# Convolution and max-pool on one core: whole-bank seeds in step 1, an earlier turn of G1, and step 3's difference ahead of step 2's sum

## The chip, the cores and the metric

The kernel runs on one core of a Trainium2 chip. The metric is the device time of one execution in microseconds (us). The engines are TensorE (PE, with its weight loads as PEld), VectorE (DVE), ScalarE (ACT), GpSimd (POOL) and SyncE (SP), which only issues DMAs here. SBUF is the on-chip working memory and PSUM the memory that TensorE accumulates into, in eight banks.

## The reference, cut to what matters

```python
batch, c_in, h, w, c_out, k = 16, 64, 64, 64, 128, 3      # pool_size 2, float32
x_pad = np.pad(x, ((0, 0), (0, 0), (1, 1), (1, 1)))
conv[b, co] += weight[co, ci, kh, kw] * x_pad[b, ci, kh:kh+h, kw:kw+w]   # over ci, kh, kw
output[b, c, i, j] = max of conv[b, c, 2*i:2*i+2, 2*j:2*j+2]
```

A 3x3 convolution with a border of zeros, 64 channels to 128, and after it the largest value of each 2x2 square.

## The kernel before

**Tiles.** Two images lie in SBUF one above the other: image 0 of a pair in partitions 0 to 63, image 1 in 64 to 127 (`h` is 0 or 1 in the code). The work has 32 steps. A step is 16 rows of such a pair of images, that is 8 pairs of rows, and makes one PSUM bank of 8 x 64 results for each image and each kind of sum. TensorE multiplies 64 rows of weights for the image above and 64 for the image below at the same time, so its matmuls come in pairs.

**Two rows at a time.** The row filter is rewritten so that an even and an odd row of the convolution share a sum. Seven blocks of turned weights are needed for it: the filter's rows G0, G1, G2, their differences D0 and D2, and GM and GP, half of G0 - G1 + G2 and half of G0 + G1 + G2. Each block is made in `wq`, turned by TensorE into a PSUM bank (`T` followed by the block: `turn`, L157, with three or four transposes at L162) and copied to `wt` (`V` followed by the block: `turn_out`, L168, whose lines L173 to L179 say which engine copies).

**Two kinds of steps** (`TYPES`). A K step casts its rows to bf16 (`kx`) and needs their sum by pairs, `ks` (KS, L294, VectorE: both operands in SBUF). A W step takes its float rows (`wx`) and needs three tiles: the difference by pairs, `we` (E, L325: on VectorE for steps 3, 4, 6 and 11, on GpSimd for the others; step 1's in halves Ea and Eb, L346, on VectorE), the differences of neighbours, `wd` (D, L334, GpSimd; step 1's in halves Da and Db, L361), and the sum by pairs, `ws` (WS, L308 as a reduction or L316 as an addition, VectorE). Each step has for each image an accumulator `ta` and an accumulator `tb`:

- K: PA1 and PA2 go to `ta`, PB1 and PB2 to `tb`. EV copies `ta` to SBUF (`ev`, L392, ScalarE). MX takes the maximum of `tb` and `ev` into `tb` (L420, VectorE). Then PR adds the product of `ks` to `tb`.
- W: P2 (with `we`) goes to `ta`. SE, the seed, copies `ta` to `tb` (L404, ScalarE). P0 goes on to `ta` and P3 to `tb` (both with `wd`). EV copies `ta`, negated (L394). MX takes the maximum, and P1 adds the product of `ws`.
- Both: OD copies the odd columns to SBUF (L424, ScalarE), CM takes the maximum of the even and the odd columns (L430, VectorE), and the store of a step is issued on SP.

The first two steps are cut in halves of four rows. F stands for step 0's products, and G for step 1's: G.0.0 and G.0.1 are the two halves of its P2, G.1 its P0 and G.2 its P3. Step 1's seeds are made in halves as well (SEa and SEb: `seed_half`, L406, with the copy at L416).

**Order.** Nothing is scheduled by a program: the string `ORDER` (L487) lists the steps one after the other, and each engine executes its own in that order. An entry is a name, a step and an image (KS.2, MX.1.0). A product waits in a queue until the other image has one too, and then the two are issued in turns. Banks come from a list, `free`; a bank is freed when its tile has been copied out. GpSimd's sums and differences are held by an added dependency (`on_gpsimd`, L78) until the last VectorE instruction that was noted ahead of them in `ORDER` (`on_vector`, L74: KS, E on VectorE, additions of WS and the like) has ended:

```python
def on_gpsimd(inst):
    behind(inst, sbuf_op[0])
    return inst
```

The first loads are issued at the start, the others by L, LB (SP) and LK (GpSimd) in `ORDER`.

Of the kernel before, what the change touches and what calls it, by code (L numbers as in the profile page):

```python
# [11 lines left out]
def kernel(  # L12
# [9 lines left out]
    nc = tc.nc  # L22
# [11 lines left out]
    R = HO // NQ  # L34
# [9 lines left out]
    WSTEPS = [s for s in range(N) if TYPES[s] == "W"]  # L44
# [17 lines left out]
    acc = [psum.tile([128, R, W], FP32, name=f"acc_{i}") for i in range(8)]  # L62
    free = deque(range(8))
    unset = set(range(8))
# [60 lines left out]
    zeros = const.tile([128, 512], BF16)  # L125
# [10 lines left out]
    D0, G2, D2, G0, G1, GM, GP = BLOCKS.values()  # L136
# [14 lines left out]
    def turned_cols(m):  # L151
        lo = BLOCKS[m] - (m in LEADING)
        hi = BLOCKS[m] + 3
        tp = acc[turned[m]].rearrange("p a b -> p (a b)").bitcast(BF16)
        return lo, hi, tp[:, 0 : (hi - lo) * CO]
# [12 lines left out]
    def turn_out(m):  # L168
        free.append(turned[m])
        lo, hi, src = turned_cols(m)  # L170
        dst = wt[:, lo:hi, :].rearrange("p a b -> p (a b)")
        if m == "GM":
            nc.scalar.mul(dst, src, 0.5)  # L173
        elif m == "GP":
            nc.vector.tensor_scalar_mul(out=dst, in0=src, scalar1=0.5)
        elif m in ("G0", "G1", "G2"):
            nc.scalar.copy(out=dst, in_=src)
        else:
            nc.vector.tensor_copy(out=dst, in_=src)  # L179
# [32 lines left out]
    ta, tb = {}, {}  # L212


    def take(where, s, h, fresh=True):
        t = next((t for t in free if fresh or t not in unset), free[0])
        free.remove(t)
        where[s, h] = t
        return t
# [134 lines left out]
    def wd_half(part):  # L354
        s = WSTEPS[0]
        if part == 0:
            row["wd", s] = d_pool.tile([128, 2 * R, W], BF16, name="wd")
        t, f = wx_rows(s)
        lo, hi = f + R * part, f + R * (part + 1)
        on_gpsimd(  # L360
            nc.gpsimd.tensor_tensor(  # L361
                out=row["wd", s][:, R * part : R * (part + 1), :],
                in0=t[:, lo + 1 : hi + 1, :],
                in1=t[:, lo - 1 : hi - 1, :],
                op=SUB,
            )
        )
# [35 lines left out]
            )  # L403
        nc.scalar.copy(out=acc[t], in_=acc[ta[s, h]])  # L404

    def seed_half(part, h):  # L406
        s = WSTEPS[0]
        span = slice(R // 2 * part, R // 2 * (part + 1))
        if part == 0:
            t = take(tb, s, h, fresh=False)  # L410
            if t in unset:
                unset.discard(t)
                nc.tensor.matmul(
                    acc[t], zeros[:, 0:128], zeros, start=True, stop=True, skip_group_check=True
                )
        nc.scalar.copy(out=acc[tb[s, h]][:, span, :], in_=acc[ta[s, h]][:, span, :])  # L416

    def rowmax(s, h):
        t = acc[tb[s, h]]
        nc.vector.tensor_tensor(out=t, in0=t, in1=ev[s, h], op=MAX)  # L420
# [27 lines left out]
    def cast_more(first):  # L448
# [24 lines left out]
        "Eb": lambda: we_half(1),  # L473
        "Da": lambda: wd_half(0),
        "Db": lambda: wd_half(1),
        "SEa": lambda h: seed_half(0, h),
        "SEb": lambda h: seed_half(1, h),
        "KS": ks, "WS": ws, "E": we, "D": wd, "L": wload, "LB": late_load, "LK": lk,
        "SE": seed, "EV": evac, "MX": rowmax, "OD": odd, "CM": colmax,
    }  # L480
    for m in BLOCKS:
        steps["T" + m] = lambda m=m: turn(m)
        steps["V" + m] = lambda m=m: turn_out(m)
    for m in PRODUCTS:
# [1 line left out]

    ORDER = """  # L487
        D0 g2 TD0 g0 D2 GS TG2 g1 VD0 PR.0.1 XEa TD2 VG2 PA1.2.1 TG0 F.2.0 VD2 XOa LB.3 LB.4 LB.6 LB.8 LB.9
        GM VG0 F.3.0 XOb F.0.0 F.1.0 TGM F.0.1 PA2.2.1 XEb LK.0.0 F.1.1 F.2.1 F.3.1 VGM GP
        Ea KS.0 Eb EV.0.1 G.0.0 EV.0.0 TG1 VG1 G.0.1 P2.3.1 SEa.0 SEa.1 SEb.1 MX.0.1 Da Db TGP SEb.0 MX.0.0 VGP  # L490
        LK.0.1 X2 PR.0.0 G.1.0 X1 G.2.0 PB1.2.1 PB2.2.1 WS.1 G.2.1 G.1.1 L.11 P0.3.1 PA1.2.0 PA2.2.0 P3.3.1
        OD.0.0 OD.0.1 EV.1.0 KS.2 E.3 CM.0.1 EV.1.1 P1.1.1 D.3 CM.0.0 PR.2.1 PB1.2.0 P2.3.0 MX.1.0 PB2.2.0
        EV.2.1 P1.3.1 SE.3.1 EV.2.0 WS.3 MX.1.1 P1.1.0 SE.3.0 P0.3.0 MX.2.0 MX.2.1 EV.3.1 PR.2.0 EV.3.0 D.4
        MX.3.1 OD.2.0 PA1.5.1 OD.1.0 E.4 PA1.5.0 PA2.5.0 P3.3.0 OD.1.1 OD.2.1 L.12 L.14 PA2.5.1 OD.3.1
        P2.4.1 CM.1.1 CM.2.0 P2.4.0 CM.1.0 PA1.7.1 D.6 EV.5.0 CM.3.1 CM.2.1 MX.3.0 PA2.7.1 PB1.5.1 SE.4.0
# [92 lines left out]
```

## Time and profile before

| | |
|---|---|
| median of 3 runs | 104.4 us (104.28 to 104.41) |
| the profiled execution | 104.27 us |
| its span, first to last instruction | 102.5 us |
| mean granted TensorE clock | 0.989 |
| busy: PE, DVE, ACT, POOL | 94%, 90%, 80%, 73% of the span |

A line of the profile's timeline has the start in us from the beginning of the span, the length in us, the engine, the line of the kernel, the operation, the tile written and the tiles read, their shapes, and the number of instructions that are merged in it. In brackets stands the idle time of the engine ahead of it and what ended that. "x2" lines reach from the start of the first to the end of the last. TensorE's ends are modelled, so its starts are the better measure. Consecutive instructions of an engine overlap a little: the next one starts up to 0.1 us before the end of the last.

### The profile page before, as it was taken

Reading aid. Unit: us, or ns where it says so; the run is one execution under the profiler, and the core shown is the slowest. Engines: PE = TensorE matmul, PEld = TensorE weight load, DVE = VectorE, ACT = ScalarE, POOL = GpSimd, SP = SyncE. Lnnn points to the kernel's source line nnn. Section 1 sums busy time; section 2 is a strip of 40 time slices with the busy share of each in tenths; the row PEclk is TensorE's granted clock in tenths of the full one; section 3 lists DMA queues with packets and bytes.
Section 4 is the critical chain, followed back from the end, with each engine's and each line's share of the span. In section 5 each row is a group of like instructions: output and inputs, shape, how many; then the busy total and the mean of one; then the engine's idle time right before and its main releaser. Section 6 shows DMA issues by size and latency. Waiting matters only on the chain.

```text
span 102.5 us, 2545 instructions
## 1 busy us (share of the span) xinstructions
PE 96.8 (94%) x908; PEld 62.7 (61%) x908; DVE 92.5 (90%) x178; ACT 82.3 (80%) x182; POOL 74.8 (73%) x61
## 2 busy tenths in 40 slices
PE   6989999999999999999999999999999999999930
PEld 2476544555865465587777885556745888865500
DVE  1498799999999999999999999999989999987970
ACT  5638988896689997993887898987899899598740
POOL 6227579764995899998999997969997928990000
PEclk9999999999999999999999999999999999999995
DMA  2999999999999999998878995097899451116044
GB/s 67 300 353 266 367 318 289 396 406 343 195 211 310 294 329 308 319 345 210 173 188 252 255 363 187 20 205 265 191 164 225 138 184 51 51 51 203 8 156 151
DMA packets 13421, 23.34 MB, mean 228 GB/s; under 512 B 1120, under 2 KB 9568, under 8 KB 13408
## 3 DMA queue, kind: packets, MB, share of 16 engines
q1 hardware_dynamic: 12400, 20.68, 62.0%
q0 software_dynamic: 864, 2.36, 14.0%
q8 instruction: 7, 0.11, 0.5%
q10 hardware_dynamic: 144, 0.13, 0.4%
q14 instruction: 6, 0.05, 0.1%
HBM read 17.14 MB, written 8.39 MB: 249 GB/s over the span
## 4 chain that ended last, share of the span: by engine, by line
PE 91%; DVE 2%; ACT 2%; issue 1%; DVEq 0%
PE acc L193 86%; PE acc L545 3%; PE acc L162 1%; DVE acc L420 1%; ACT acc L416 1%; ACT od L424 1%; ACT ev L394 0%; DVE wt L179 0%; DVE o L430 0%; DVE kx L446 0%; DVEq L583 0%
## 5 line engine op out<-in xcount | busy, mean ns | idle before, releaser
L193 PEld LDWEIGHTS <-wt 64*128 64x128 bf16 x876 | 60.1, 94 | 31.5 <-issue 1.9
L334 POOL TENSOR_TENSOR wd<-wx 128x1024 bf16<-128x1024 f32 x20 | 47.0, 2356 | 8.3 <-PE acc L193 3.4
L193 PE MATMUL acc<-kx,wt 64*128 64x504 bf16 (+6 forms) x288 | 50.2, 356 | 0.4 <-DVE kx L446 0.4
L193 PE MATMUL acc<-wd,wt 64*128 64x504 bf16 (+3 forms) x264 | 50.0, 367 | 0.2 <-ACT acc L416 0.2
L420 DVE TENSOR_TENSOR acc<-acc,ev 128x512 f32<-128x512 f32 x64 | 41.9, 691 | 1.5 <-PE acc L193 0.8
L193 PE MATMUL acc<-we,wt 64*128 64x512 bf16 (+2 forms) x132 | 31.9, 367 | 0.0
L193 PE MATMUL acc<-ws,wt 64*128 64x504 bf16 (+1 forms) x126 | 28.7, 377 | 0.2 <-DVE acc L420 0.2
L424 ACT COPY od<-acc 128x256 f32<-128x256 f32 x64 | 22.7, 379 | 6.3 <-PE acc L193 5.8
L394 ACT ACTIVATE ev<-acc 128x512 f32<-128x512 f32 x42 | 25.0, 609 | 2.4 <-PE acc L193 2.1
L430 DVE TENSOR_TENSOR o<-acc,od 128x256 f32<-128x256 f32 x64 | 24.7, 416 | 1.1 <-ACT od L424 0.9
L404 ACT COPY acc<-acc 128x512 f32<-128x512 f32 x40 | 23.0, 581 | 3.0 <-PE acc L193 1.7
L325 POOL TENSOR_TENSOR we<-wx 128x512 bf16<-128x512 f32 x16 | 20.2, 1269 | 3.3 <-DVE ws L316 2.4
L193 PE MATMUL acc<-ks,wt 64*128 64x504 bf16 (+1 forms) x66 | 16.5, 377 | 0.1
L308 DVE TENSOR_REDUCE ws<-wx 128x512 bf16<-128x1024 f32 x12 | 14.8, 1231 | 0.0
L392 ACT COPY ev<-acc 128x512 f32<-128x512 f32 x22 | 12.9, 595 | 0.7 <-PE acc L193 0.7
L316 DVE TENSOR_TENSOR ws<-wx 128x512 bf16<-128x512 f32 x9 | 6.7, 763 | 0.0
L294 DVE TENSOR_TENSOR ks<-kx 128x512 bf16<-128x512 bf16 x11 | 4.6, 426 | 0.5 <-ACT kx L453 0.5
L96 POOL DMA_DIRECT2D kx<-in_x_dram x6 | 3.5, 588 | 1.8 <-DVE kx L446 1.8
L545 PE MATMUL acc<-const-bfloat16-1.0 128*128 128x512 bf16 x8 | 3.6, 628 | 0.8 <-PEq L569 0.8
L361 POOL TENSOR_TENSOR wd<-wx 128x512 bf16<-128x512 f32 x2 | 2.5, 1264 | 0.8 <-DVE we L346 0.8
L325 DVE TENSOR_TENSOR we<-wx 128x512 bf16<-128x512 f32 x4 | 2.7, 683 | 0.0
L460 DVE TENSOR_TENSOR wq<-wraw 128x192 bf16<-128x192 f32 x1 | 0.5, 500 | 2.4 <-DMA wraw<-in_weight_dram 2.4
(29 smaller groups left out, 20.1 us busy)
## 6 DMA issues: line engine op xcount, KB each, us to landing
out_dram<-o SPq DMA_DIRECT2D x26, 256.0 KB, 5.0
wx<-in_x_dram SPq DMA_DIRECT2D x10, 512.0 KB, 7.1
wx<-in_x_dram SPq DMA_DIRECT2D x5, 544.0 KB, 7.5
wx<-in_x_dram SPq DMA_DIRECT2D x5, 480.0 KB, 7.5
out_dram<-o SPq DMA_DIRECT2D x11, 128.0 KB, 2.0
kx<-in_x_dram POOLq DMA_DIRECT2D x2, 528.0 KB, 7.8
ksecond<-in_x_dram SPq DMA_DIRECT2D x1, 512.0 KB, 6.2
kx<-in_x_dram POOLq DMA_DIRECT2D x2, 256.0 KB, 7.0
```

Source lines behind the costliest of these rows:

```text
L193: nc.tensor.matmul(acc[t][:, i0:i1, o0:o1], wt[lo : lo + CI, m0 + kw - h, :], rows(lo, i0, i1, c0, c1), start=start and kw == 1, stop=True ...
L308: nc.vector.tensor_reduce(out=row["ws", s], in_=t[:, f : f + 2 * R, :].rearrange("p (r two) w -> p r w two", two=2), axis=mybir.AxisListTy ...
L316: nc.vector.tensor_tensor(out=row["ws", s], in0=t[:, f : f + 2 * R : 2, :], in1=t[:, f + 1 : f + 2 * R : 2, :], op=ADD)
L325: inst = (nc.vector if vector else nc.gpsimd).tensor_tensor(out=row["we", s], in0=t[:, f : f + 2 * R : 2, :], in1=t[:, f + 1 : f + 2 * R : ...
L334: nc.gpsimd.tensor_tensor(out=row["wd", s], in0=t[:, f + 1 : f + 1 + 2 * R, :], in1=t[:, f - 1 : f - 1 + 2 * R, :], op=SUB)
L392: nc.scalar.copy(out=ev[s, h], in_=acc[t])
L394: nc.scalar.mul(ev[s, h], acc[t], -1.0)
L404: nc.scalar.copy(out=acc[t], in_=acc[ta[s, h]])
L420: nc.vector.tensor_tensor(out=t, in0=t, in1=ev[s, h], op=MAX)
L424: nc.scalar.copy(out=od[s, h], in_=acc[tb[s, h]][:, :, 1::2])
L430: nc.vector.tensor_tensor(out=ot[s][:, h], in0=acc[t][:, :, 0::2], in1=od[s, h], op=MAX)
L545: nc.tensor.matmul(acc[n].rearrange("p a b -> p (a b)"), ones[:, 0:128], ones, start=True, stop=True, skip_group_check=True)
```

## The change

Three things change.

1. Step 1's seeds copy a whole bank (SE.1.0, SE.1.1 with `seed`) where they copied two halves each; `seed_half` and its two entries go.
2. TG1, the turn of G1, stands next to TGM, ahead of most of step 0's F products, and not between the two halves of step 1's P2. Its copy to `wt`, VG1, is VectorE's and no longer ScalarE's, and stands behind Eb.
3. E.3 stands directly behind EV.1.0, and KS.2 behind CM.0.0. So the order on VectorE is E.3, CM.0.1, CM.0.0, KS.2, where it was KS.2, E.3, CM.0.1, CM.0.0. D.3 on GpSimd keeps its place between the two CM, and is still held until E.3's end.

TensorE has the same instructions as before, VectorE one more, ScalarE three fewer, and GpSimd and SP keep theirs in the same order. D.4, which was held behind E.3, is now held behind KS.2. Three banks (88, 89 and 90) change places with each other from step 1's P2 on.

```diff
@@ turn_out
-        elif m in ("G0", "G1", "G2"):
+        elif m in ("G0", "G2"):
             nc.scalar.copy(out=dst, in_=src)
         else:
             nc.vector.tensor_copy(out=dst, in_=src)
@@
-    def seed_half(part, h):
-        s = WSTEPS[0]
-        span = slice(R // 2 * part, R // 2 * (part + 1))
-        if part == 0:
-            t = take(tb, s, h, fresh=False)
...
-        nc.scalar.copy(out=acc[tb[s, h]][:, span, :], in_=acc[ta[s, h]][:, span, :])
@@ steps
-        "SEa": lambda h: seed_half(0, h),
-        "SEb": lambda h: seed_half(1, h),
@@ ORDER
-        GM VG0 F.3.0 XOb F.0.0 F.1.0 TGM F.0.1 PA2.2.1 XEb LK.0.0 F.1.1 F.2.1 F.3.1 VGM GP
-        Ea KS.0 Eb EV.0.1 G.0.0 EV.0.0 TG1 VG1 G.0.1 P2.3.1 SEa.0 SEa.1 SEb.1 MX.0.1 Da Db TGP SEb.0 MX.0.0 VGP
+        GM VG0 F.3.0 XOb F.0.0 F.1.0 TGM TG1 F.0.1 PA2.2.1 XEb LK.0.0 F.1.1 F.2.1 F.3.1 VGM GP
+        Ea KS.0 Eb VG1 EV.0.1 G.0.0 EV.0.0 G.0.1 P2.3.1 SE.1.0 SE.1.1 MX.0.1 Da Db TGP MX.0.0 VGP
         LK.0.1 X2 PR.0.0 G.1.0 X1 G.2.0 PB1.2.1 PB2.2.1 WS.1 G.2.1 G.1.1 L.11 P0.3.1 PA1.2.0 PA2.2.0 P3.3.1
-        OD.0.0 OD.0.1 EV.1.0 KS.2 E.3 CM.0.1 EV.1.1 P1.1.1 D.3 CM.0.0 PR.2.1 PB1.2.0 P2.3.0 MX.1.0 PB2.2.0
+        OD.0.0 OD.0.1 EV.1.0 E.3 CM.0.1 EV.1.1 P1.1.1 D.3 CM.0.0 KS.2 PR.2.1 PB1.2.0 P2.3.0 MX.1.0 PB2.2.0
```

More of the change, by code (lines that the diff above doesn't have):

```diff
@@ L404, in seed @@
         nc.scalar.copy(out=acc[t], in_=acc[ta[s, h]])
-    def seed_half(part, h):
-        s = WSTEPS[0]
-        span = slice(R // 2 * part, R // 2 * (part + 1))
-        if part == 0:
-            t = take(tb, s, h, fresh=False)
[L411 to L416, printed above, removed]
     def rowmax(s, h):
```

## The prediction

> **What bounds the kernel now.** I read the page's busy shares and chain first, then the chain in order of time, then the timelines of TensorE, VectorE, ScalarE and GpSimd from 7 to 18 us, where every edit lies.
>
> From the page, the busy shares and the chain; then a piece of the chain in order of time (start, length, what):
>
> ```profile
> PE 96.8 (94%) x908; PEld 62.7 (61%) x908; DVE 92.5 (90%) x178; ACT 82.3 (80%) x182; POOL 74.8 (73%) x61
> PE 91%; DVE 2%; ACT 2%; issue 1%; DVEq 0%
> ...
> 11.31 64.26 PE acc L193 x604
> ```
>
> From 11.31 us on, TensorE is the chain for 64 us without a break, and for another 20 us after a gap of 0.02. So a wait of TensorE gained or lost before about 20 us reaches the end one for one, as long as nothing later waits on something that doesn't shift with it. Two such waits stand in the opening: for VectorE's maxima at 10.30 and for ScalarE's seeds at 11.31. TensorE's timeline (start, length, engine, line):
>
> ```profile
> 8.66 0.49 PE L193 MATMUL acc<-we,wt 64*128 64x256 bf16 x6
> 9.09 0.34 PE L162 MATMUL acc<-ident,wq 128*128 128x128 bf16 x3
> 9.36 0.50 PE L193 MATMUL acc<-we,wt 64*128 64x256 bf16 x6
> 9.80 0.40 PE L162 MATMUL acc<-ident,wq 128*128 128x128 bf16 x4
> 10.30 0.82 PE L193 MATMUL acc<-ks,wt 64*128 64x512 bf16 x6
> 11.31 1.49 PE L193 MATMUL acc<-wd,wt 64*128 64x256 bf16 x24 [0.18 <-ACT acc L416]
> ```
>
> The same stretch of VectorE, and under it GpSimd:
>
> ```profile
> 8.95 1.30 DVE L420 TENSOR_TENSOR acc<-acc,ev 128x512 f32<-128x512 f32 x2 [0.39 <-PE acc L193]
> 10.23 0.42 DVE L175 TENSOR_SCALAR wt<-acc 128x512 bf16<-128x512 bf16 x1
> 10.57 1.24 DVE L308 TENSOR_REDUCE ws<-wx 128x512 bf16<-128x1024 f32 x1
> 12.33 0.42 DVE L294 TENSOR_TENSOR ks<-kx 128x512 bf16<-128x512 bf16 x1 [0.52 <-ACT kx L453]
> 12.67 0.68 DVE L325 TENSOR_TENSOR we<-wx 128x512 bf16<-128x512 f32 x1
> 13.28 0.75 DVE L430 TENSOR_TENSOR o<-acc,od 128x256 f32<-128x256 f32 x2
> 13.94 0.69 DVE L420 TENSOR_TENSOR acc<-acc,ev 128x512 f32<-128x512 f32 x1
> 14.54 1.23 DVE L308 TENSOR_REDUCE ws<-wx 128x512 bf16<-128x1024 f32 x1
> 15.69 2.51 DVE L420 TENSOR_TENSOR acc<-acc,ev 128x512 f32<-128x512 f32 x4
> ```
>
> ```profile
> 13.45 4.67 POOL L334 TENSOR_TENSOR wd<-wx 128x1024 bf16<-128x1024 f32 x2 [1.78 <-DVE we L325]
> ```
>
> The order matters here: KS.2 (12.33) runs while GpSimd computes nothing, E.3 follows, and only E.3's end lets D.3 start at 13.45.
>
> **The opening: the turn of G1 and the seeds.** Pairs of 256 columns start 0.11 us apart (twelve from 7.34 to 8.66). TG1 between G.0.0 and G.0.1 makes the way from one to the other 0.70 us (8.66 to 9.36) where three pairs take 0.33, so taking it out saves 0.37. Next to TGM it adds three transposes at 0.06 (four take 0.40, three 0.34), 0.17. The F products thus end 0.17 later, G.0.1 starts at 8.66 + 0.17 + 0.33 = 9.16, not 9.36, and TGP 0.20 earlier.
>
> The first maximum waits for the last F product: 8.95 becomes 9.12, the two end at 10.25 + 0.17 = 10.42, and PR.0 starts 0.05 later as now, at 10.47. VG1 on VectorE costs nothing there: after Eb (8.14 + 0.42 = 8.56) the engine idles until 8.95, later 9.12, and a copy of this shape from PSUM takes 0.33 (at 5.54). The bound from the other side: GpSimd's Da starts at 8.65, beside it. But VD0's copy ran under GpSimd's GS (4.82, 0.42 us) and VGP under Db (10.23, 0.42), both of the same length, so I take 0.33. Without that cover VG1 would push PR.0 by up to 0.33.
>
> On ScalarE VG1's 0.48 goes, and four half copies (1.30) become two whole ones: 1.06, as two evacuations of the same shape take 1.07. The seeds start 0.59 after G.0.1 starts (9.36 to 9.95), so at 9.75, and end at 10.81. G.1.0 no longer waits for them but for PR.0's three pairs, 0.65 us (17.20 to 17.85): 10.47 + 0.65 = 11.12 instead of 11.31. Gain of the opening: 0.19 us.
>
> **E.3 ahead of KS.2.** VectorE now runs VGP at 10.40, WS.1 at 10.74, and the next starts 1.15 after it (14.54 to 15.69): E.3 at 11.89, not 12.67, ending 12.57. Its rows are issued at 6.10 and take 5.5 us to land, 11.6: in time by 0.3. D.3 waits for E.3 alone and starts 0.09 after it, as now: 12.66, ending 15.01 (2.35). CM.0.1 and CM.0.0 follow E.3 at 12.49 (0.61 after its start, as now). Their odd columns are there: ScalarE's casts follow the seeds at 10.71 (0.10 before their end, as at 11.15 now), the copies of the odd columns start 1.04 after that (11.15 to 12.19) and take 0.66, until 12.41. KS.2's turn comes at 12.49 + 0.66 = 13.15, and then GpSimd is in the middle of D.3.
>
> KS.2 reads two operands in SBUF. What the trace shows of such an instruction when it comes to its turn under a GpSimd TENSOR_TENSOR (VectorE rows, then the GpSimd rows they fell under):
>
> ```profile
> 66.69 0.49 DVE L294 TENSOR_TENSOR ks<-kx 128x512 bf16<-128x512 bf16 x1
> 77.78 1.05 DVE L316 TENSOR_TENSOR ws<-wx 128x512 bf16<-128x512 f32 x1
> ```
>
> ```profile
> 65.62 1.28 POOL L325 TENSOR_TENSOR we<-wx 128x512 bf16<-128x512 f32 x1
> 75.93 2.35 POOL L334 TENSOR_TENSOR wd<-wx 128x1024 bf16<-128x1024 f32 x1
> ```
>
> Alone, L294 takes 0.42 and L316 0.68. Here they take 0.07 and 0.37 more, with 0.21 and 0.50 us of GpSimd's instruction still to run. A third (L316 at 73.69, 0.85 us) takes 0.17 more with 0.30 to run. In each case the excess is that remainder less about 0.13: they end 0.28 (L294) and 0.55 (L316) after GpSimd's end, as if they had stood still until 0.13 before it. At half speed the one at 77.78 would have lost at most 0.25. Maxima (one operand in PSUM) and TENSOR_REDUCE (one operand) under the same GpSimd instructions keep their lengths, 0.69 and 1.23. So KS.2's excess lies between 0.37, the longest that a row shows, and the whole rest of D.3 less 0.13, 1.72. I take the second, because the three rows follow the remainder and not a fixed price: KS.2 ends at 15.01 + 0.28 = 15.29.
>
> The Trainium skill, "SBUF — State Buffer", section "Who interferes with whom", says that a VectorE instruction with two SBUF inputs contends with a GpSimd one that reads SBUF, and that the one that comes second is blocked fully, not throttled. By it the sum is the same, 105.5; by the longest wait shown alone it would be 104.2. The trace agrees as far as its rows go; none holds for longer than 0.37.
>
> Behind KS.2 on VectorE stand the maxima. MX.1.0 starts 0.08 before KS.2's end, at 15.21 (now 13.94); then by the present spacings (0.60, 1.15, 0.60) WS.3 15.81, MX.1.1 16.96, MX.2.0 17.56, ending 18.25. TensorE: P1.1.1 needs MX.1.0's bank. Its turn is 15.87 - 0.19 = 15.68, and it gets it at 15.90 + 0.05 = 15.95: a wait of 0.27. PR.2.0, now at 17.20, comes up 1.33 later, at 17.28, and needs MX.2.0: 18.25 + 0.05 = 18.30, a wait of 1.02. After it the other two maxima end at 18.85 and 19.47, ahead of their readers (18.95, 19.60), so no third wait.
>
> **What else moves.** D.3's reader, P0.3.1, has its rows at 15.01 instead of 15.80, worth nothing, as it stands in the same pair as P1.1.1. D.4 is now held until KS.2's end and starts at 15.38 (now 15.77): no loss. E.4, two SBUF operands too, comes at 19.4, clear of D.4's end at 17.7. D.6 follows E.4 and runs until 22.5, and KS.7, at 21.26 + 1.10, meets its last 0.1: nothing. The store of step 0 and L.12 and L.14 behind it on SP go 0.8 earlier; GpSimd's own DMA issues keep their place up to LK.0.1 and shift with VectorE afterwards. Loads in flight get readers that come 1.1 later. Banks 88 to 90 swap names only.
>
> **Sum:** -0.19 + 0.27 + 1.02 = +1.10 us. The profiled execution took 104.27 with a span of 102.5, so 105.37 with 103.6; it lay 0.13 under the median of 104.40, so the forecast is 105.5.
>
> **Rivals.** (A) KS.2 is held little: not slower. If it ends by 14.00, held under 0.43 us, MX.2.0 is ready when TensorE's turn comes at 17.01, and only the opening's gain is left: 104.40 - 0.19 = 104.2. For it: no row shows a longer hold than 0.37. Against it: all three follow the remainder. 0.06.
>
> (B) Part is given back later. VectorE is busy 90% and TensorE 94%, and TensorE has small waits near the end. Against it: these follow VectorE and ScalarE instructions that follow TensorE itself, and none is for a landing. Half given back: 104.95. 0.09.
>
> (C) E.3's rows land later than 11.89, and VectorE stands there with the whole chain behind it, one for one. For it: the margin is 0.3 us, where it was 1.1, and the next load took 6.4 us, which here would be 12.5, +0.6, 106.1. Against it: nothing ahead of that issue changes. 0.07.
>
> (D) The forecast, 105.5, 0.78. Its own spread is the maxima's start (0.1) and what 80 us of shifted overlaps between VectorE's sums and GpSimd add or spare (0.2): 105.2 to 105.8.
>
> **The numbers.** The range 104.9 to 105.9 takes D, B and the smaller half of C, and leaves out A and the rest. 0.2% is 0.21 us, about what a measurement of this kernel can tell from no change. A lies on that border and is split, 0.03 and 0.03, and 0.01 each is added for what I have not seen: faster 0.04, same 0.04, slower 0.92.
>
> **What would show it.** In the profile after: KS.2 as an L294 row of about 2.1 us from 13.15 that ends 0.28 after D.3; D.3 starting near 12.7; PR.0 at 10.47 and the first wd products at 11.12; TensorE idle shortly before 18.3, released by VectorE's maximum, and the chain passing there through VectorE and GpSimd. A KS.2 of 0.4 to 0.8 us makes A right and the forecast wrong; E.3 starting after 12 with a landing as its releaser is C.

## The result, and the profile after

The changed kernel is slower. Its median is 105.33 us (105.19 to 105.83, 6 runs) against 104.39 (104.25 to 104.42, 6 runs); the ratio is 1.0103, with a 95% interval of 1.0082 to 1.0124. The profiled execution took 105.33 us with a span of 103.6, 1.06 more than that of before.

The page's busy shares and chain, and a piece of the chain in order of time (start, length, what), all of after:

```profile
PE 96.8 (93%) x908; PEld 63.7 (62%) x908; DVE 94.2 (91%) x179; ACT 81.5 (79%) x179; POOL 74.8 (72%) x61
PE 79%; DVE 10%; DMA 4%; issue 2%; ACT 1%; SPq 0%; DVEq 0%
...
11.92 0.60 DVE we L325
12.51 0.70 DVE o L418 x2
13.22 2.02 DVE ks L294
...
18.25 58.39 PE acc L193 x537
```

TensorE is busy as long as before (96.8 us), so nothing was added to its work. The chain now passes through VectorE, from 9.15 to 18.21 us, where before it was TensorE's from 11.31 on. Its longest piece there is KS.2. The same stretch in VectorE's timeline, then GpSimd's (the line numbers behind `seed_half` are 12 lower):

```profile
11.84 0.68 DVE L325 TENSOR_TENSOR we<-wx 128x512 bf16<-128x512 f32 x1
12.46 0.76 DVE L418 TENSOR_TENSOR o<-acc,od 128x256 f32<-128x256 f32 x2
13.13 2.10 DVE L294 TENSOR_TENSOR ks<-kx 128x512 bf16<-128x512 bf16 x1
15.16 0.69 DVE L408 TENSOR_TENSOR acc<-acc,ev 128x512 f32<-128x512 f32 x1
15.76 1.23 DVE L308 TENSOR_REDUCE ws<-wx 128x512 bf16<-128x1024 f32 x1
16.91 2.48 DVE L408 TENSOR_TENSOR acc<-acc,ev 128x512 f32<-128x512 f32 x4
```

```profile
12.61 2.35 POOL L334 TENSOR_TENSOR wd<-wx 128x1024 bf16<-128x1024 f32 x1 [1.14 <-DVE we L325]
15.32 2.37 POOL L334 TENSOR_TENSOR wd<-wx 128x1024 bf16<-128x1024 f32 x1 [0.37 <-DVE ks L294]
```

KS.2, 0.42 us long before, is a row of 2.10 us. It comes to its turn half a microsecond after D.3's start (12.61) and ends 0.29 after D.3 does, by the trace; its operation and its shapes are the same. D.4 (15.32) now waits for it. TensorE's timeline, with the wait that follows:

```profile
10.51 0.82 PE L193 MATMUL acc<-ks,wt 64*128 64x512 bf16 x6 [0.48 <-DVE acc L408]
11.15 1.49 PE L193 MATMUL acc<-wd,wt 64*128 64x256 bf16 x24
...
15.90 0.37 PE L193 MATMUL acc<-ws,wt 64*128 64x512 bf16 x1
...
18.25 0.37 PE L193 MATMUL acc<-ks,wt 64*128 64x512 bf16 x1 [0.88 <-DVE acc L408]
```

The first wd products start at 11.15 and not at 11.31, so the opening did gain. PR.2.0 starts at 18.25 and not at 17.20, behind the maximum of its bank.

### The profile page after: what moved, and what is told of

Its sections match the earlier page's. It is cut to its first block, busy times and chain, and to the rows that moved or that the text cites. A ratio compares the mean times of both kernels' runs of the same rounds, so it can differ in the third digit from the quotient of the medians.

```text
span 103.6 us, 2545 instructions
## 1 busy us (share of the span) xinstructions
PE 96.8 (93%) x908; PEld 63.7 (62%) x908; DVE 94.2 (91%) x179; ACT 81.5 (79%) x179; POOL 74.8 (72%) x61
## 4 chain that ended last, share of the span: by engine, by line
PE 79%; DVE 10%; DMA 4%; issue 2%; ACT 1%; SPq 0%; DVEq 0%
PE acc L193 79%; DVE acc L408 4%; DMA kfirst<-in_x_dram 4%; DVE ks L294 2%; DVE ws L308 1%; DVE o L418 1%; ACT od L412 1%; DVE we L325 1%; ACT ev L394 0%; PE acc L162 0%; DVE kx L434 0%; SPq L110 0%; DVEq L569 0%; DVE wt L175 0%; DVEq L408 0%
## 5 line engine op out<-in xcount | busy, mean ns | idle before, releaser
L193 PEld LDWEIGHTS <-wt 64*128 64x128 bf16 x876 | 61.1, 94 | 31.7 <-issue 3.4
L404 ACT COPY acc<-acc 128x512 f32<-128x512 f32 x42 | 24.1, 582 | 3.4 <-PE acc L193 1.7
L294 DVE TENSOR_TENSOR ks<-kx 128x512 bf16<-128x512 bf16 x11 | 6.3, 576 | 0.0
```

The costliest lines, as they stand in the source:

```text
L193: nc.tensor.matmul(acc[t][:, i0:i1, o0:o1], wt[lo : lo + CI, m0 + kw - h, :], rows(lo, i0, i1, c0, c1), start=start and kw == 1, stop=True ...
L294: nc.vector.tensor_tensor(out=row["ks", s], in0=t[:, f : f + 2 * R : 2, :], in1=t[:, f + 1 : f + 2 * R : 2, :], op=ADD)
```

## The experiments

The theory: KS.2 reads two operands in SBUF and stands still as long as GpSimd's D.3 runs. The rivals: the loss comes with the turn of G1 and the seeds, which put VectorE's maxima later; or with E.3's place; or any VectorE instruction at that place would be held.

TGM starts at 7.01 to 7.14 us in six of the ten profiles and at 7.39 to 7.53 in the other four (KS.2 back ahead, KS.2 with one operand, D.3 behind KS.2, D.3 in halves). The difference arises ahead of everything that was changed: in those four TensorE works at about half its later pace until 6.4 to 6.6 us, with the pairs of F 0.18 to 0.22 us apart, and 0.11 from then on; in the others the pairs are 0.11 apart from the first or the second on. In three of the four the profiled execution is also 0.28 to 0.32 us above the median of its kernel. So the table counts from the start of TGM. "First wd" is G.1.0's first matmul, and "last product" is TensorE's last matmul. KS.2's end is given against D.3's, negative where KS.2 ends first. The ratios are of execution times, with all that varies in them.

| kernel | first wd | KS.2, length | KS.2's end minus D.3's | PR.2.0 | last product | ratio to before (95%) |
|---|---|---|---|---|---|---|
| before | 4.30 | 0.42 | -3.04 | 10.19 | 91.05 | 1 |
| after | 4.09 | 2.10 | +0.29 | 11.19 | 92.09 | 1.0103 (1.0082 to 1.0124) |
| KS.2 back ahead | 4.09 | 0.42 | -3.04 | 9.98 | 90.87 | 0.9983 (0.9971 to 0.9995) |
| the order alone | 4.30 | 1.57 | +0.29 | 11.14 | 92.00 | 1.0084 (1.0065 to 1.0102) |
| KS.2 with one operand | 4.09 | 1.21 | -0.62 | 10.29 | 91.23 | 1.0023 (1.0010 to 1.0035) |
| D.3 behind KS.2 | 4.09 | 0.42 | -2.44 | 9.98 | 90.91 | 0.9985 (0.9968 to 1.0002) |
| D.3 in halves | 4.09 | 1.02 | +0.28 (its first half) | 10.10 | 91.04 | 1.0023 (1.0000 to 1.0046) |
| whole seeds alone | 3.93 | 0.42 | -3.05 | 9.92 | 90.80 | 0.9975 (0.9959 to 0.9991) |
| the turn alone | 4.09 | 0.42 | -3.18 | 9.98 | 90.88 | 0.9997 (0.9985 to 1.0009) |
| the turn in the gap | 3.93 | 0.42 | -3.04 | 9.82 | 90.68 | 0.9980 (0.9963 to 0.9997) |

### KS.2 back ahead of E.3

```diff
-        OD.0.0 OD.0.1 EV.1.0 E.3 CM.0.1 EV.1.1 P1.1.1 D.3 CM.0.0 KS.2 PR.2.1 ...
+        OD.0.0 OD.0.1 EV.1.0 KS.2 E.3 CM.0.1 EV.1.1 P1.1.1 D.3 CM.0.0 PR.2.1 ...
```

> The changed kernel with KS.2 back ahead of E.3; the turn of G1 and the whole-bank seeds stay. Hold theory (KS.2 stood still under D.3 until 0.13 us before its end): KS.2 is a row of 0.42 us near 11.93, E.3 starts at 12.27 and D.3 at 13.04, TensorE waits nowhere between 11.15 and 20 us, and only the opening's gain is left, 0.16 us by the trace of after (11.31 to 11.15): 104.2 us. Rival (the loss came with the turn of G1 or the seeds, which put VectorE's maxima 0.2 later): it stays, 105.3 us.

Measured: 104.27 us, ratio 0.9983 (0.9971 to 0.9995). VectorE's row of KS.2:

```profile
12.36 0.42 DVE L294 TENSOR_TENSOR ks<-kx 128x512 bf16<-128x512 bf16 x1
```

The whole loss is gone with this one move, and the opening's gain appears in the time. That rules out the turn and the seeds as its cause.

### The order alone, in the kernel before

```diff
-        OD.0.0 OD.0.1 EV.1.0 KS.2 E.3 CM.0.1 EV.1.1 P1.1.1 D.3 CM.0.0 PR.2.1 ...
+        OD.0.0 OD.0.1 EV.1.0 E.3 CM.0.1 EV.1.1 P1.1.1 D.3 CM.0.0 KS.2 PR.2.1 ...
```

> The kernel before with E.3 ahead of KS.2 and nothing else changed. Hold theory: E.3 at 11.72, D.3 at 12.49 to 14.84, KS.2 comes up near 13.6, under D.3, and ends at 15.12, the first of step 1's maxima starts at 15.04, that of step 2 ends at 18.08, and PR.2.0 starts at 18.13 and not at 17.20: +0.93, 105.3 us, the same as the whole change, so that the opening's gain is hidden behind the hold. Rival (parts add up: -0.16 from the opening and the rest from the order): 105.5 us. Rival (no hold): 104.4 us.

Measured: 105.29 us, ratio 1.0084. VectorE's row of KS.2 and GpSimd's row of D.3:

```profile
13.66 1.57 DVE L294 TENSOR_TENSOR ks<-kx 128x512 bf16<-128x512 bf16 x1
```

```profile
12.60 2.35 POOL L334 TENSOR_TENSOR wd<-wx 128x1024 bf16<-128x1024 f32 x1 [1.12 <-DVE we L325]
```

Here KS.2 comes up half a microsecond later than in after, and its row is half a microsecond shorter; both end 0.29 after D.3 by the trace. So it is the end of D.3 that counts and not a fixed price. PR.2.0 is as late as in after, within 0.05, although the opening gained nothing: the hold hides what the opening gives.

### KS.2 with one operand

Step 2's K sum as a reduction over pairs of rows, as the float rows of some W steps are summed; the same sums, at the same place. As it is not noted by `on_vector`, D.4 is held until E.3's end and no longer until KS.2's.

```diff
+        if s == 2:
+            with nc.allow_low_precision("bf16 operand of TensorE, as the other row sums"):
+                nc.vector.tensor_reduce(
+                    out=row["ks", s],
+                    in_=t[:, f : f + 2 * R, :].rearrange("p (r two) w -> p r w two", two=2),
+                    axis=mybir.AxisListType.X,
+                    op=ADD,
+                )
+            return
```

> The changed kernel with KS.2 as a reduction over pairs (one operand in SBUF, the same sums), at the same place under D.3. Hold theory (only two operands in SBUF are held): a row near 1.23 us from 13.13, as the reductions of the float rows, not held; step 1's first maximum at 14.28, step 2's ends at 17.32, PR.2.0 at 17.37 where 17.04 would be its turn: -0.16 + 0.33 = +0.17, 104.6 us, though the instruction itself is 0.8 us longer. Rival (whatever VectorE runs with two reads of bf16 rows under D.3 is held): a row of about 2.9 us that ends 1.1 after D.3, and 106.2 us.

Measured: 104.65 us, ratio 1.0023 (1.0010 to 1.0035). VectorE's row, and GpSimd's D.3 and D.4 as one row; KS.2 lies under the first:

```profile
13.61 1.21 DVE L295 TENSOR_REDUCE ks<-kx 128x512 bf16<-128x1024 bf16 x1
```

```profile
13.08 4.68 POOL L343 TENSOR_TENSOR wd<-wx 128x1024 bf16<-128x1024 f32 x2 [1.49 <-DVE we L334]
```

An instruction three times as long, with one operand, ends 0.62 before D.3, and the kernel is faster with it than with the short one with two (104.65 and 105.33 us). This is the run that tells the hold from the rival that anything at that place is held. The reduction is also another operation; that this isn't what counts is shown by the rows of after, where CM.0.0 has the operation of KS.2 (TENSOR_TENSOR) but one of its operands in PSUM: it starts at 12.80, under D.3, and takes 0.41 us. So of what VectorE runs there, only the instruction with two operands in SBUF is held.

### D.3 behind KS.2

```diff
-        OD.0.0 OD.0.1 EV.1.0 E.3 CM.0.1 EV.1.1 P1.1.1 D.3 CM.0.0 KS.2 PR.2.1 ...
+        OD.0.0 OD.0.1 EV.1.0 E.3 KS.2 CM.0.1 EV.1.1 P1.1.1 D.3 CM.0.0 PR.2.1 ...
```

> The changed kernel with KS.2 directly behind E.3, so that D.3 is held until KS.2 has ended; E.3 is still first. Hold theory: KS.2 0.42 us at 12.43, D.3 from 12.94 to 15.29, ahead of its reader's turn at 15.71, no wait of TensorE: 104.2 us, as with KS.2 back ahead. Rival (E.3 ahead is the trouble, since it stands for its rows or delays the odd columns' maxima): 104.5 us or more.

Measured: 104.22 us, ratio 0.9985 (0.9968 to 1.0002). GpSimd's row of D.3 and D.4, the first now released by KS.2:

```profile
13.32 4.67 POOL L334 TENSOR_TENSOR wd<-wx 128x1024 bf16<-128x1024 f32 x2 [1.78 <-DVE ks L294]
```

E.3 stays ahead of KS.2, and the hold is gone; PR.2.0 stands where it stands with KS.2 back ahead. So E.3's place is not the trouble: what costs is that D.3 was let go while VectorE still had an instruction with two operands to come.

### D.3 in halves

```diff
+        if s == 3:
+            for lo in (f, f + R):
+                on_gpsimd(
+                    nc.gpsimd.tensor_tensor(
+                        out=row["wd", s][:, lo - f : lo - f + R, :],
+                        in0=t[:, lo + 1 : lo + 1 + R, :],
+                        in1=t[:, lo - 1 : lo - 1 + R, :],
+                        op=SUB,
+                    )
+                )
+            return
```

> The changed kernel with D.3 as two instructions of half the rows (1.26 us each, as step 1's), the rest as it is. Hold theory (a hold lasts until 0.13 before the end of the GpSimd instruction that is running, and then VectorE's has its turn): first half 12.61 to 13.87, KS.2 comes up at 13.13 and ends at 14.15, a row of 1.0 us; the second half runs after it, to about 15.4, ahead of its reader's turn at 15.71; step 1's first maximum at 14.07, step 2's ends at 17.11 and PR.2.0 starts at 17.16 where 17.04 would be its turn: -0.16 + 0.12, 104.4 us, no change. Rival (the second half, already queued, goes ahead of KS.2): KS.2 still ends after 15.2, and 105.4 us.

VectorE's KS.2, then GpSimd's two halves as one row, from the timeline; the last line is from the view of GpSimd's line L336 (shortest, median and longest, in ns):

```profile
13.47 1.02 DVE L294 TENSOR_TENSOR ks<-kx 128x512 bf16<-128x512 bf16 x1
```

```profile
12.94 2.67 POOL L336 TENSOR_TENSOR wd<-wx 128x512 bf16<-128x512 f32 x2 [1.44 <-DVE we L325]
```

```profile
L336 POOL TENSOR_TENSOR wd<-wx x2: 1266/1352/1437, 12.9 to 14.2; 128x512 bf16<-128x512 f32 x2
```

The row is 1.02 us, as expected: KS.2 waited for the first half only, and went ahead of the second, which was queued. Counted from TGM, PR.2.0 lies 0.09 earlier than in before, and the last product 0.02 earlier: no change, as expected. The time agrees less well: 104.66 us where 104.4 was expected, ratio 1.0023 (1.0000 to 1.0046), with executions from 104.10 to 105.33. In the profiled one (104.61) the excess over before's (104.27) comes from TensorE's slower start: its TGM comes 0.38 later, ahead of all that was changed here. What made the executions above 105 us so long is not settled.

### The parts of the opening

Whole-bank seeds alone, in the kernel before:

```diff
-        ... TG1 VG1 G.0.1 P2.3.1 SEa.0 SEa.1 SEb.1 MX.0.1 Da Db TGP SEb.0 MX.0.0 VGP
+        ... TG1 VG1 G.0.1 P2.3.1 SE.1.0 SE.1.1 MX.0.1 Da Db TGP MX.0.0 VGP
```

> The kernel before with the whole-bank seeds alone; the turn of G1, its copy on ScalarE, and KS.2 ahead of E.3 as before. If the opening's limit is ScalarE's chain: VG1 ends at 9.95, the two seeds at 11.01 (1.06 in place of 1.30), and the first wd products start at 11.07 in place of 11.31, as PR.0 still starts at 10.30: -0.24, 104.2 us. Rival (seeds are off the path, the gain was the turn's): 104.4 us.

Measured: 104.12 us, ratio 0.9975 (0.9959 to 0.9991). TensorE's two rows, and ScalarE's seeds:

```profile
10.38 0.83 PE L193 MATMUL acc<-ks,wt 64*128 64x512 bf16 x6
11.03 1.59 PE L193 MATMUL acc<-wd,wt 64*128 64x256 bf16 x24
```

```profile
10.04 1.06 ACT L404 COPY acc<-acc 128x512 f32<-128x512 f32 x2
```

The first wd product gains more than I expected, 0.37 and not 0.24 counted from TGM: it starts right behind PR.0, at 11.03, while the second seed ends only at 11.10. Of this, 0.26 to 0.27 are left at PR.2.0 and at the last product. A whole-bank seed lets image 0's products start when its own bank is copied; with halves in the order a.0, a.1, b.1, b.0, image 0 was released last. Whether halves with image 0's first would do the same was not run.

The turn of G1 and VG1 on VectorE alone, in the kernel before:

```diff
-        elif m in ("G0", "G1", "G2"):
+        elif m in ("G0", "G2"):
@@
-        ... F.1.0 TGM F.0.1 ... Ea KS.0 Eb EV.0.1 G.0.0 EV.0.0 TG1 VG1 G.0.1 ...
+        ... F.1.0 TGM TG1 F.0.1 ... Ea KS.0 Eb VG1 EV.0.1 G.0.0 EV.0.0 G.0.1 ...
```

> The kernel before with the turn of G1 next to that of GM and VectorE's copy alone; half-bank seeds, and KS.2 ahead of E.3 as before. PR.0 starts at 10.50 as in after (the F products and the maxima are 0.2 later), the four half copies end near 11.08, and the first wd products start at 11.15 in place of 11.31, by PR.0 and no longer by the seeds: -0.16, 104.25 us. With the whole-bank seeds (KS.2 back ahead) it was 104.27, so the whole seeds would add nothing to the turn. Rival (the parts add up: whole seeds 0.24 of which the turn gives none): 104.4 us.

Measured: 104.36 us, ratio 0.9997 (0.9985 to 1.0009). In the trace the first wd products are 0.21 earlier, counted from TGM, just as with both parts (4.09 in both), so the whole seeds add nothing once the turn has moved. Nor does the earlier turn add anything to the whole seeds: the first wd products are at 3.93 with the seeds alone and at 4.09 with both, as PR.0 then waits for the later F products and maxima. The last product is 0.18 earlier than in before, but the time can't tell this gain from none.

### The turn in TensorE's gap

```diff
-        D0 g2 TD0 g0 D2 GS TG2 g1 VD0 PR.0.1 XEa TD2 VG2 PA1.2.1 TG0 F.2.0 VD2 ...
-        GM VG0 F.3.0 ...
+        D0 g2 TD0 g0 D2 GS TG2 g1 VD0 PR.0.1 XEa TD2 VG2 PA1.2.1 TG0 TG1 F.2.0 VD2 ...
+        GM VG0 VG1 F.3.0 ...
-        ... EV.0.0 TG1 VG1 G.0.1 P2.3.1 SEa.0 SEa.1 SEb.1 MX.0.1 Da Db TGP SEb.0 MX.0.0 VGP
+        ... EV.0.0 G.0.1 P2.3.1 SE.1.0 SE.1.1 MX.0.1 Da Db TGP MX.0.0 VGP
```

> The kernel before with whole-bank seeds and the turn of G1 ahead of step 0's first product, in TensorE's idle time before 5.67 (it waits there for VectorE's cast), with VG1 on ScalarE behind VG0, where that idles until 7.44; KS.2 ahead of E.3 as before. If idle time hides both: F products, maxima and PR.0 as before (10.30), G.0.1 at 8.99 and not 9.36, seeds 9.58 to 10.64, the first wd products right behind PR.0 at 10.95: -0.36, 104.05 us, faster than before and than the changed kernel with KS.2 back. Rival (the copy of G1 on ScalarE or the seventh bank delays step 0's first products): 104.4 us or more.

Measured: 104.06 us, ratio 0.9980 (0.9963 to 0.9997), faster than before and than after. TensorE's rows, and ScalarE's three copies in its own idle time:

```profile
4.33 1.40 PE L162 MATMUL acc<-ident,wq 128*128 128x128 bf16 x16
5.76 1.41 PE L193 MATMUL acc<-kx,wt 64*128 64x256 bf16 x24
...
10.39 0.82 PE L193 MATMUL acc<-ks,wt 64*128 64x512 bf16 x6 [0.48 <-DVE acc L420]
11.04 1.49 PE L193 MATMUL acc<-wd,wt 64*128 64x256 bf16 x24
```

```profile
5.26 1.24 ACT L177 COPY wt<-acc 128x384 bf16<-128x384 bf16 x3 [0.17 <-PE acc L162]
```

The turn costs nothing in the gap: step 0's products start at 5.76, where the whole seeds alone, without the turn there, start them at 5.75. What is left in the opening is 0.48 us ahead of PR.0, which waits for VectorE's maxima. Against the whole seeds alone the further gain (PR.2.0 at 9.82 and not 9.92) is inside the intervals.

## Why the prediction was right

**The opening** was put at -0.19, with PR.0 at 10.47 and the first wd products at 11.12. The profile of after has 10.51 and 11.15, -0.16; counted from TGM, which came 0.05 later for reasons ahead of the change, it is -0.21. VG1 on VectorE (8.28, 0.35 us) lay ahead of the maxima's start (9.15) and cost nothing, as said. The step held; the parts behind it were less well known than the sum: the whole seeds bring at least as much by themselves (3.93 against 4.09 for the first wd), by releasing image 0's bank earlier, which the prediction did not see, and the turn's place next to TGM adds nothing to them.

**E.3 and D.3** were put at 11.89 and 12.66; they started at 11.84 and 12.61. The rows had landed in time, so rival (C) did not come up in this execution.

**The hold** was the term that decided, and its size was taken from the remainder of GpSimd's instruction and not from the longest excess that a row of before shows (0.37). That step was right: KS.2 took 1.68 more than its 0.42, where 1.72 was forecast from the whole of D.3's rest; the order alone and the halves gave 1.15 and 0.60 more with less of GpSimd's instruction to run, each ending 0.28 to 0.29 after it. To go from 0.37 to 1.72 was to carry three rows far beyond their lengths; the runs bear it out at 0.60, 1.15 and 1.68. Rival (A), no long hold, is out. The rule of the Trainium skill ("SBUF — State Buffer", "Who interferes with whom") agrees with these three at lengths that the trace of before could not show, and with the reduction, which was not held.

**TensorE's waits** were put at 0.27 for P1.1.1 and 1.02 for PR.2.0. From the profile they are 0.19 (its turn would have been 15.87 - 0.16 = 15.71, it got it at 15.90) and 1.02 (15.90 + 1.33 = 17.23, and 18.25). The sum, -0.16 + 0.19 + 1.02, is 1.05, the 18.25 - 17.20 of the two profiles. The terms are not independent: with the order alone the opening gains nothing, the waits are shorter by about as much, and PR.2.0 comes at the same time within 0.05, counted from TGM. The profiled executions differ by 1.06, the medians by 0.94. The forecast for the profiled execution was 105.37 and it took 105.33; the 0.13 that was added to reach the median of before did not come back in after, whose profiled execution is its median.

**Given back later** (rival B): no. TensorE's last product, counted from TGM, comes 1.04 later than in before (92.09 and 91.05 us), so what was lost by 18 us arrives at the end.

## What to carry to other kernels

For every VectorE instruction with two operands in SBUF, look for what GpSimd is running when its turn comes. A hold is not shown as idle time: the row shows the remainder of GpSimd's instruction as VectorE's own length. Moving a short sum behind an instruction that releases a long one on GpSimd can cost most of the long one: here 1.68 us of D.3's 2.35 in the row, and about 1 us of the kernel's time. So let the release wait for the short one, which here cost nothing that the times can tell, or give the sum one operand, which made it 0.8 us longer itself. A small piece of work for an engine on the path belongs in a wait that is already there: the turn of G1 cost nothing in TensorE's idle time before its first product.

## What the runs showed of the hardware

The hold ends before GpSimd's recorded end. In after, with the order alone and with D.3 in halves, KS.2 ended 0.28 to 0.29 us after it, though it takes 0.42 by itself, so it seems to have begun 0.13 to 0.14 us before it.

I had not expected a sign of the hold working the other way in the same run. With D.3 in halves, the second half, queued behind the first, started in the record 0.3 us before KS.2 ended and took 1.44 us where the first took 1.27: VectorE's waiting instruction went ahead, and GpSimd's row was 0.17 longer. That it was held for this time is the nearest reading; one run shows it, and no other tests it.

TensorE's pace in the first 6.6 us differs from one execution to the next. In D.3 in halves the first pairs of F start at 5.80, 5.99, 6.20 and 6.39 us and the later ones 0.11 apart; in before they are 0.11 apart from the first pair on. The granted clock that the profile gives for 4.8 to 6.4 us is 1.00 in both, so it doesn't tell the two apart. What decides the pace is open.
